# Seven quarter products in place of eight for the down products of three MLPs

## The chip, the core and the metric

The kernel runs on one NeuronCore of a Trainium2 chip as a single program. The metric is the device time of one execution in microseconds, from runs of the same program. Five engines work side by side, each through its own list of instructions in order: TensorE (PE, matmuls, with its weight loads shown apart as PEld), VectorE (DVE), ScalarE (ACT), GpSimd (POOL) and SyncE (SP, which here only issues DMAs).

## The reference

The reference is a small stack of transformer blocks on 512 tokens of width 1024, all in float32: a gated linear recurrence, a differential attention, a state-space mixer beside a windowed attention, and a cross attention. Three of the blocks end in an MLP, and only these matter here:

```python
def squared_relu_mlp(h, w_up, w_down):
    u = jax.nn.relu(h @ w_up)
    return (u * u) @ w_down
```

`w_up` is 1024 x 4096 and `w_down` 4096 x 1024. The first two MLPs are followed by an RMS norm with a gain and added to the residual; the third is added to the residual directly, and a last norm follows.

## The kernel before

Every large matrix product is made from float32 operands that are split in two rounded parts, high and low (type fp32r). `mm3` (line 398) multiplies a pair by a pair with three matmuls: high by high, high by low, low by high. For a split, ACT rounds the source to the high part and DVE subtracts it from the source to get the low part: `Weights._split` (lines 119 and 121) for weights, `split` (lines 407 and 408) for activations.

Weights pass through the class `Weights` (line 64). `specs` lists every unit of weights in the order of use; a unit is cut in parts of 128 x 1024 elements (512 KB). SP loads a part into one of three raw buffers, and the split writes one of six `hl` buffers. When the program asks for unit i (`get`, line 148), `ahead` splits parts until six of them from the start of unit i on are under way, and loads three parts further. An up unit and each half of a quarter product below is two parts.

`mlp` (line 586) treats the 4096 features in four blocks of 1024. In a block, four up units give 8 tiles of 128 features by 512 tokens: 24 matmuls of 128x128 against 128x512 each, into a PSUM buffer of the pool `ps_m` (three banks). `up_evac` takes the relu on ACT into `rl`, the square on DVE into `sq`, and splits it into the stationary operands `uk(0)` to `uk(7)`, which lie in `UAh`, `UAl`, `UBh` and `UBl`. Then the block's down product follows. For the first three blocks it is `tok2` (line 539), once for each half of the 1024 output columns: for each of four token tiles, 8 k steps of `mm3` into one PSUM buffer, and `add_to` (line 563) adds the result to `acc` or, in the third MLP, to `h` (in the first block of the first two MLPs ACT copies it):

```python
for u in range(2):
    cs = slice(u * 512, (u + 1) * 512)
    tok2(WT.get(f"{pre}dn{q}{u}"), uk, lambda t, ps: add_to(dst[:, t, cs], ps, post and q == 0))
```

The fourth block does the first half of its features in the same way and ends with `last_rows` (line 549), token tile by token tile, so that the norm that follows (`after`) can begin. `load_gp` (line 569) loads the gain row of that norm into the buffer `GP`, issued by ACT ahead of the MLP.

The order of instructions on each engine isn't the order of the program text. The framework plays the program against its own model of time when it builds it and lists for each engine, at each moment, the earliest instruction of the text that is ready in that model. On the chip each list then runs strictly in order, with semaphore waits.

Of the kernel before, what the change touches and what calls it, by code (L numbers as in the profile page):

```python
# [66 lines left out]
class Weights:  # L67


    def __init__(s, nc, raw_p, spl_p, specs, live, raws):  # L70
        s.nc, s.raw_p, s.spl_p, s.specs, s.live, s.raws = nc, raw_p, spl_p, specs, live, raws
        s.half = [(i, j) for i, sp in enumerate(specs) for j in range(s._parts(sp))]
        s.first = []
        n = 0
        for sp in specs:
            s.first.append(n)
            n += s._parts(sp)
        s.first.append(n)
        s.raw, s.hl = {}, {}
        s.n_dma = s.n_spl = s.n_get = 0  # L80
# [6 lines left out]
    @staticmethod  # L87
    def _rows(sp):
        return min(sp[1], 1024 // sum(c[3] for c in sp[2]))

    def _dma(s, q):
        i, j = s.half[q]
        name, nk, cols = s.specs[i][:3]
        w = sum(c[3] for c in cols)
# [11 lines left out]
        s.raw[q] = v  # L106

    def _split(s, q):
# [3 lines left out]
        w = sum(c[3] for c in cols)  # L112
        r = s.raw.pop(q)
# [25 lines left out]
    def load(s, n):  # L139
        for i in range(n):  # L140
            s._dma(s.n_dma)
            s.n_dma += 1
# [55 lines left out]
def body(ctx, tc, I, out, dbg=None, stop=None):  # L198
# [39 lines left out]

    def mlp_specs(pre, up, down):
# [158 lines left out]
    def mm3(ps, a, b, first, last):  # L398
        nc.tensor.matmul(ps, a[0], b[0], start=first, stop=False)  # L399
        nc.tensor.matmul(ps, a[0], b[1], start=False, stop=False)  # L400
        nc.tensor.matmul(ps, a[1], b[0], start=False, stop=last)  # L401
# [27 lines left out]
    def ev_y():  # L429
        return st["ev"].tile([P, D], F32, tag="y", name="y")  # L430
# [155 lines left out]
    def mlp(pre, post, after):  # L586
        wk = st["wk"]
        wk.phase()
        dst = acc if post else h

        def up_evac(u):
            def f(n, ps):
# [3 lines left out]
                sq = wk.get("sq", 512, 3)  # L596
# [3 lines left out]

        for q in range(4):
            us = 0
            if q == 0:
                i0 = WT.n_get
                ws = [WT.get(f"{pre}up00"), WT.get(f"{pre}up01", hold=i0)]
                feat_first(ws, xk, [up_evac(0), up_evac(1)])
                us = 2
            for u in range(us, 4):
                feat(WT.get(f"{pre}up{q}{u}"), xk, up_evac(u))
# [267 lines left out]
    load_gp(I["mlp_norm_post"][0])  # L877
# [10 lines left out]
    mlp("m0", True, after1)  # L888
# [149 lines left out]
    load_gp(I["mlp_norm_post"][1])  # L1038
# [13 lines left out]
    mlp("m1", True, after3)  # L1052
# [471 lines left out]
    load_gp(I["norm_final_2"])  # L1524
# [17 lines left out]
    mlp("m2", False, after6)  # L1542
# [30 lines left out]
```

## Time and profile before

| | us |
|---|---|
| median of three runs | 2620.57 (2620.28 to 2620.72) |
| the profiled execution | 2621.18 |
| its span, first to last instruction | 2619.3 |

| engine | busy us | share of the span | instructions |
|---|---|---|---|
| PE | 2552.2 | 97% | 13064 |
| PEld | 2130.0 | 81% | 13064 |
| DVE | 1481.6 | 57% | 2841 |
| ACT | 1142.4 | 44% | 2136 |
| POOL | 184.9 | 7% | 199 |

Busy time counts the time in which an engine has at least one instruction under way. Matmuls overlap each other, so the sum of their durations is larger than PE's busy time, and what a matmul costs is read from the distance of starts. Waits are listed with the instruction that ended them. 249.79 MB were moved by DMA.

### The profile page before, as it was taken

How to read it: one execution, taken by the hardware profiler on the slowest of the kernel's cores; microseconds unless marked ns; L12 is line 12 of the kernel's file. 1: busy time of each engine (PE TensorE's matmuls, PEld its weight loads, DVE VectorE, ACT ScalarE, POOL GpSimd, SP SyncE). 2: the span in 40 equal slices, each digit the busy share in tenths (PEclk: the TensorE clock that was granted, in tenths of full speed). 3: DMA queues.
4: the chain of work that ended last, by engine and by line, in shares of the span. 5: the costliest groups of instructions: out<-in, count | busy, mean ns of one | idle time of the engine just before them, and what ended most of it. 6: DMA issues, size and time to landing. Idle time of an engine off the chain costs nothing. (4 is left out here: it accounts for less than half of the span.)

```text
span 2619.3 us, 33641 instructions
## 1 busy us (share of the span) xinstructions
PE 2552.2 (97%) x13064; PEld 2130.0 (81%) x13064; DVE 1481.6 (57%) x2841; ACT 1142.4 (44%) x2136; POOL 184.9 (7%) x199
## 2 busy tenths in 40 slices
PE   8999999999999989999999999998999999999998
PEld 7888788888888768888887778787887788888887
DVE  5566653344666654333477788887555466534434
ACT  6333343233466553322356654563555336423322
POOL 1100210000201030000031100010000000100000
PEclk9999999999999999999999999998999999999999
DMA  5522233223222122332333433352221233222221
GB/s 179 154 65 65 81 105 96 88 96 99 88 89 89 65 89 88 105 95 82 105 117 112 110 105 109 104 145 79 72 73 32 89 97 121 81 97 97 97 97 57
DMA packets 187310, 249.79 MB, mean 95 GB/s; under 512 B 9936, under 2 KB 126912, under 8 KB 187152
## 3 DMA queue, kind: packets, MB, share of 16 engines
q1 hardware_dynamic: 175664, 207.97, 25.2%
q0 software_dynamic: 10192, 34.96, 5.0%
q10 hardware_dynamic: 1296, 4.72, 0.5%
q8 instruction: 103, 1.69, 0.3%
q14 instruction: 55, 0.45, 0.1%
HBM read 243.25 MB, written 9.61 MB: 97 GB/s over the span
## 5 line engine op out<-in xcount | busy, mean ns | idle before, releaser
L400 PE MATMUL psm<-XTl,hl 128*128 128x512 f32 (+1 forms) x1400 | 537.6, 384 | 7.8 <-DVE XTl L408 7.8
L399 PE MATMUL psm<-XTh,hl 128*128 128x512 f32 (+1 forms) x1400 | 534.8, 383 | 5.9 <-ACT XTh L407 5.1
L401 PE MATMUL psm<-XTh,hl 128*128 128x512 f32 (+1 forms) x1400 | 534.5, 382 | 0.0
L119 ACT ACTIVATE hl<-raw 128x1024 fp32r<-128x1024 f32 x321 | 338.4, 1056 | 425.5 <-PE psm L401 361.3
L121 DVE TENSOR_TENSOR hl<-raw,hl 128x1024 fp32r<-128x1024 f32 x305 | 374.9, 1231 | 247.9 <-ACT hl L119 244.8
L400 PEld LDWEIGHTS psm<-XTl,hl 128*128 128x128 f32 x1400 | 266.9, 191 | 57.1 <-DVE XTl L408 8.6
L399 PEld LDWEIGHTS psm<-XTh,hl 128*128 128x128 f32 x1400 | 266.0, 190 | 55.4 <-ACT XTh L407 6.1
L401 PEld LDWEIGHTS psm<-XTh,hl 128*128 128x128 f32 x1400 | 266.6, 190 | 48.8 <-issue 0.2
L399 PE MATMUL psm<-hl,UAh 128*128 128x512 f32 x640 | 255.9, 400 | 5.0 <-DVE WS L1130 1.8
L400 PE MATMUL psm<-hl,UAh 128*128 128x512 f32 x640 | 251.0, 392 | 0.0
L401 PE MATMUL psm<-hl,UAl 128*128 128x512 f32 x640 | 251.0, 395 | 0.0
L399 PE MATMUL psm<-hl,XTh 128*128 128x512 f32 (+1 forms) x640 | 231.2, 362 | 4.1 <-ACT XTh L407 3.2
L400 PE MATMUL psm<-hl,XTh 128*128 128x512 f32 (+1 forms) x640 | 229.8, 359 | 0.0
L401 PE MATMUL psm<-hl,XTl 128*128 128x512 f32 (+1 forms) x640 | 229.2, 358 | 0.0
L399 PE MATMUL psm<-hl,UBh 128*128 128x512 f32 (+1 forms) x512 | 202.2, 395 | 1.2 <-ACT UBh L410 0.8
L400 PE MATMUL psm<-hl,UBh 128*128 128x512 f32 (+1 forms) x512 | 200.6, 392 | 0.0
L401 PE MATMUL psm<-hl,UBl 128*128 128x512 f32 (+1 forms) x512 | 198.4, 390 | 0.0
L597 DVE TENSOR_TENSOR WK<-WK,psm 128x512 f32<-128x512 f32 x90 | 61.8, 687 | 171.4 <-ACT WK L595 171.4
L595 ACT ACTIVATE WK<-psm 128x512 f32<-128x512 f32 x90 | 53.9, 599 | 226.7 <-PE psm L401 226.7
L567 DVE TENSOR_TENSOR ACC<-psm,ACC 128x512 f32<-128x512 f32 x112 | 75.9, 686 | 134.9 <-PE psm L401 134.5
L399 PEld LDWEIGHTS psm<-hl,UAh 128*128 128x128 f32 x640 | 121.1, 189 | 33.7 <-DVE ACC L567 3.0
L401 PEld LDWEIGHTS psm<-hl,UAl 128*128 128x128 f32 x640 | 120.5, 188 | 27.0 <-issue 0.7
(415 smaller groups left out, 4016.0 us busy)
## 6 DMA issues: line engine op xcount, KB each, us to landing
raw<-in_mlp_w_up_dram SPq DMA_DIRECT2D x64, 512.0 KB, 3.9
raw<-in_mlp_w_down_dram SPq DMA_DIRECT2D x64, 512.0 KB, 3.3
raw<-in_w_in_dram SPq DMA_DIRECT2D x60, 512.0 KB, 3.7
WS<-aD POOLq DMA_DIRECT2D x32, 512.0 KB, 6.1
raw<-in_w_up_dram SPq DMA_DIRECT2D x32, 512.0 KB, 3.7
raw<-in_w_down_dram SPq DMA_DIRECT2D x32, 512.0 KB, 3.6
raw<-in_w_in_dram SPq DMA_DIRECT2D x33, 256.0 KB, 3.2
raw<-in_a_w_in_dram SPq DMA_DIRECT2D x16, 512.0 KB, 5.6
```

The source lines that it names most:

```text
L119: s.nc.scalar.activation(out=h, in_=r, func=AF.Copy)
L121: eng.tensor_tensor(out=l, in0=r, in1=h.bitcast(F32), op=ALU.subtract)
L399: nc.tensor.matmul(ps, a[0], b[0], start=first, stop=False)
L400: nc.tensor.matmul(ps, a[0], b[1], start=False, stop=False)
L401: nc.tensor.matmul(ps, a[1], b[0], start=False, stop=last)
L567: nc.vector.tensor_tensor(out=dst, in0=ps, in1=dst, op=ALU.add)
L595: nc.scalar.activation(out=rl, in_=ps, func=AF.Relu)
L597: nc.vector.tensor_tensor(out=sq, in0=rl, in1=ps, op=ALU.mult)
```

## The change

For the first three blocks of each MLP, the down product C = A B (A: 512 tokens x 1024 features, B: 1024 features x 1024 columns) is cut in quarters A11 to A22 and B11 to B22, and the four quarters of C come from seven products of quarters:

- P1 = A11 B11; P2 = A12 B21
- P5 = (A22 - A21)(B11 + B12); P6 = (A21 - A22 - A11)(B11 + B12 + B22)
- P7 = (A11 - A21)(B12 + B22); P3 = (A22 - A21 + A11 - A12) B22
- P4 = A22 (B11 + B12 + B22 + B21)
- C11 = P1 + P2; C22 = -P5 - (P1 + P6 + P7); C12 = -(P1 + P6) - (P5 + P3); C21 = P1 + P6 + P7 + P4

They run in the order 1, 5, 6, 2, 7, 3, 4. A product is 2 token tiles of 128 by 512 columns over 4 k steps. Products 1, 6, 7 and 4 add on in the same two PSUM banks ("a", from the pool `ps_s`), 5 and 3 in two others ("b"), and 2 has two of `ps_m` ("c"); after each product its banks are read and added to or subtracted from a quarter of `dst`.

The squares stay unsplit in `U` (4096 words of the work buffer `WK`). `left(p)` forms the left operand of product p in place in `U` on DVE where it is a sum (products 5, 6, 7 and 3) and splits it into one of `UAh`, `UAl`, `UBh`, `UBl` in turn, two parts of 1024 in each. The first is made ahead of the third up unit, three more at the start of the down product, and the others after the products 1, 5 and 6.

For the weights, each product is a unit of two parts (j = 0, 1). Products 1, 5, 2, 7 and 4 load a part into a raw buffer as before. `_hold` loads B11 into `T` (a buffer of the pool `ev` for each j) for product 5 and B22 into `B22` or `GP` for product 6, issued by SP up to five parts ahead of the raw loads. `_combine` adds the raw part to `T` (products 5 and 4), B22 to `T` (product 6) or B22 to the raw part (product 7), on DVE, before the split. As `GP` is in use, `load_gp` moves to the end of the third block.

```diff
@@ class Weights
+    def _hold(s, q):
+        u = s._sums(q)
+        if u is None:
+            return
+        (ap, k0), p = u
+        j = s.half[q][1]
+        need = {5: ((0, 0, 0),), 6: ((2, 1, 1),)}.get(p, ())
+        for (r, kh, ch) in need:
+            t = s.place(r, j)
+            r0 = (k0 + 4 * kh + 2 * j) * P
+            s.nc.sync.dma_start(
+                out=t.rearrange("p (k n) -> p k n", k=2),
+                in_=ap[r0:r0 + 2 * P, ch * 512:(ch + 1) * 512].rearrange("(k p) n -> p k n", p=P))
+            s.held[r, j] = t
+    def _combine(s, q):
+        (_, p), j = s._sums(q), s.half[q][1]
+        add = lambda a, b: s.nc.vector.tensor_tensor(out=a, in0=a, in1=b, op=ALU.add)
+        T = s.held.get((0, j))
+        if p == 6:
+            add(T, s.held[2, j])
+            return T
+        if p == 3:
+            return s.held[2, j]
+        r = s.raw.pop(q)
+        if p in (5, 4):
+            add(T, r)
+            return T
+        if p == 7:
+            add(r, s.held[2, j])
+        return r
...
     def load(s, n):
         for i in range(n):
+            while s.n_held < min(s.n_dma + 5, s.first[-1]):
+                s._hold(s.n_held)
+                s.n_held += 1
             s._dma(s.n_dma)
...
+    SEVEN = ((1, (0, 0)), (5, (0, 1)), (6, None), (2, (1, 0)), (7, (0, 1)), (3, None), (4, (1, 0)))
...
             if q < 3:
-                wide(f"{pre}dn{q}", down, q * 8, 8)
+                seven(f"{pre}dn{q}", down, q * 8)
...
-    def mlp(pre, post, after):
+    def held(r, j):
+        if r == 0:
+            return ev_y()
+        return st["GP"] if j else st["B22"]
+    def mlp(pre, post, after, gp):
...
+        U = wk.get("U", 4096).rearrange("p (k n) -> p k n", k=8)
+        st["B22"] = wk.get("B22", 1024) if post else ACC[:, 0:1024]
...
+        def up_keep(u):
+            def f(n, ps):
+                rl = wk.get("rl", 512, 3)
+                nc.scalar.activation(out=rl, in_=ps, func=AF.Relu)
+                nc.vector.tensor_tensor(out=U[:, u * 2 + n], in0=rl, in1=ps, op=ALU.mult)
+            return f
...
+        def left(p):
+            a11, a12, a21, a22 = (quarter(*i) for i in ((0, 0), (0, 1), (1, 0), (1, 1)))
+            stt = lambda o, x, y: nc.vector.scalar_tensor_tensor(out=o, in0=x, scalar=-1.0, in1=y, op0=ALU.mult, op1=ALU.subtract)
+            if p == 5:
+                nc.vector.tensor_tensor(out=a21, in0=a22, in1=a21, op=ALU.subtract)
+            elif p == 6:
+                stt(a11, a21, a11)
+            elif p == 7:
+                stt(a21, a11, a22)
+            elif p == 3:
+                stt(a12, a11, a12)
...
+            split((h_, l_), {1: a11, 5: a21, 6: a11, 2: a12, 7: a21, 3: a12, 4: a22}[p])
+            return h_, l_
+        def down7(q):
+            order = [p for p, _ in SEVEN]
+            lefts = [left(p) for p in order[1:4]]
+            lefts.insert(0, st.pop("left1"))
+            banks = {}
+            plan = {1: ("a", ((0, 0, 1),)), 5: ("b", ((1, 1, -1),)), 6: ("a", ((0, 1, -1),)), 2: ("c", ((0, 0, 1),)),
+                    7: ("a", ((1, 1, -1),)), 3: ("b", ((0, 1, -1),)), 4: ("a", ((1, 0, 1),))}
+            written = set() if post and q == 0 else {(i, j) for i in range(2) for j in range(2)}
+            for n, p in enumerate(order):
+                w = WT.get(f"{pre}dn{q}s{p}")
+                lh, ll = lefts[n]
+                b, outs = plan[p]
+                new = b not in banks
+                if new:
+                    banks[b] = [PM() if b == "c" else PS() for i in range(2)]
+                for i in range(2):
+                    ps = banks[b][i]
+                    tk = slice(i * P, (i + 1) * P)
+                    for k in range(4):
+                        mm3(ps, (lh[:, k, tk], ll[:, k, tk]), w[k], new and k == 0, k == 3, True)
+                    for (r, c, sg) in outs:
+                        d = dst[:, 2 * r + i, 512 * c:512 * c + 512]
+                        if (r, c) not in written:
+                            nc.scalar.activation(out=d, in_=ps, func=AF.Copy, scale=float(sg))
+                        else:
+                            nc.vector.tensor_tensor(out=d, in0=d, in1=ps, op=ALU.add if sg > 0 else ALU.subtract)
+                written |= {o[:2] for o in outs}
+                if n + 4 < 7:
+                    lefts.append(left(order[n + 4]))
...
             if q < 3:
-                for u in range(2):
-                    cs = slice(u * 512, (u + 1) * 512)
-                    tok2(WT.get(f"{pre}dn{q}{u}"), uk, lambda t, ps: add_to(dst[:, t, cs], ps, post and q == 0))
+                down7(q)
+                if q == 2:
+                    load_gp(gp)
```

The fourth block, the up products, the norms and all other stages stay as they are.

## Rows read from the trace of the kernel before

**Rows 1.** The page's first part: busy us (share of the span) x instructions, by engine.
```profile
PE 2552.2 (97%) x13064; PEld 2130.0 (81%) x13064; DVE 1481.6 (57%) x2841; ACT 1142.4 (44%) x2136; POOL 184.9 (7%) x199
```
**Rows 2.** The page's chain that ended last: shares by engine, then by line.
```profile
PE 30%; DVE 0%; ACT 0%; issue 0%; ACTq 0%
PE psm L399 8%; PE psm L400 8%; PE psm L401 8%; PE pss L1374 2%; PE pss L1370 1%; PE pss L1349 1%; PE pss L492 0%; PE pss L1491 0%; PE pss L401 0%; PE pss L400 0%; PE pss L399 0%; PE pss L1485 0%; PE pss L1423 0%; DVE h L567 0%; DVE XTl L408 0%
```
**Rows 3.** Stretches: us; busy (count) of PE, PEld, DVE, ACT, POOL; clock; DMA share; GB/s.
```profile
431.00:474.60 43.60, 43.60 (x194) 36.05 (x193) 20.11 (x23) 17.03 (x23) 0.00 (x0) 1.00 0.36 119
474.60:518.90 44.30, 44.30 (x193) 36.06 (x192) 14.89 (x17) 9.50 (x10) 0.00 (x0) 1.00 0.25 73
```
**Rows 4.** Timeline of ACT: start, duration, instruction, count, idle time before and releaser.
```profile
386.69 0.60 ACT L595 ACTIVATE WK<-psm 128x512 f32<-128x512 f32 x1 [1.72 <-PE psm L401]
...
404.63 1.06 ACT L119 ACTIVATE hl<-raw 128x1024 fp32r<-128x1024 f32 x1 [0.79 <-PE psm L401]
...
408.80 0.60 ACT L565 ACTIVATE ACC<-psm 128x512 f32<-128x512 f32 x1 [0.29 <-PE psm L401]
...
431.01 0.60 ACT L565 ACTIVATE ACC<-psm 128x512 f32<-128x512 f32 x1 [0.34 <-PE psm L401]
...
474.62 0.60 ACT L595 ACTIVATE WK<-psm 128x512 f32<-128x512 f32 x1 [1.72 <-PE psm L401]
```
**Rows 5.** Groups by line and form: count, busy us, mean ns, idle before, releasers.
```profile
L121 DVE TENSOR_TENSOR hl<-raw,hl 128x1024 fp32r<-128x1024 f32 x304 | 372.7, 1227 | 247.9 <-ACT hl L119 244.8
L119 ACT ACTIVATE hl<-raw 128x1024 fp32r<-128x1024 f32 x320 | 337.8, 1057 | 425.5 <-PE psm L401 361.3 <-DMA raw<-in_mlp_w_up_dram 24.8 <-DMA raw<-in_w_up_dram 13.3
L597 DVE TENSOR_TENSOR WK<-WK,psm 128x512 f32<-128x512 f32 x90 | 61.8, 687 | 171.4 <-ACT WK L595 171.4
L407 ACT ACTIVATE UBh<-WK 128x512 fp32r<-128x512 f32 x48 | 30.1, 627 | 18.1 <-DVE WK L597 18.1
L579 DVE SCALAR_TENSOR_TENSOR h<-WK,rr,h 128x1024 f32<-128x1024 f32 x3 | 3.8, 1279 | 0.2
```
**Rows 6.** Timeline of DVE, up and down stretches of the first MLP.
```profile
358.73 1.23 DVE L121 TENSOR_TENSOR hl<-raw,hl 128x1024 fp32r<-128x1024 f32 x1 [1.21 <-ACT hl L119]
359.87 0.69 DVE L408 TENSOR_TENSOR UAl<-WK,UAh 128x512 fp32r<-128x512 f32 x1
360.48 0.68 DVE L597 TENSOR_TENSOR WK<-WK,psm 128x512 f32<-128x512 f32 x1
...
493.65 2.60 DVE L121 TENSOR_TENSOR hl<-raw,hl 128x1024 fp32r<-128x1024 f32 x2 [1.79 <-ACT hl L119]
...
497.61 0.68 DVE L567 TENSOR_TENSOR ACC<-psm,ACC 128x512 f32<-128x512 f32 x1
```
**Rows 7.** Busy time by stretch: the kernel's start, and a wait before the first MLP.
```profile
0.00:65.00 65.00, 55.91 (x340) 50.60 (x341) 36.50 (x85) 42.22 (x91) 11.88 (x28) 1.00 0.58 180
340.00:350.00 10.00, 10.00 (x74) 10.00 (x74) 7.35 (x15) 4.15 (x10) 0.00 (x0) 0.84 0.30 108
```
**Rows 8.** DMA issue: count, KB each, median us from issue to landing.
```profile
raw<-in_mlp_w_up_dram SPq DMA_DIRECT2D x64, 512.0 KB, 3.9
```
**Rows 9.** Who waited for whom: us in total, times, longest.
```profile
SPq L101 <- DVE hl L121: 1603.3, 266, 62.5
...
DVE hl L121 <- ACT hl L119: 244.8, 186, 15.6
```
**Rows 10.** Timeline of PE after a wait, shortly before the first MLP.
```profile
337.45 0.58 PE L400 MATMUL psm<-XTl,hl 128*128 128x256 f32 x1 [3.20 <-DVE XTl L408]
337.83 0.41 PE L401 MATMUL psm<-XTh,hl 128*128 128x256 f32 x1
338.04 0.41 PE L399 MATMUL psm<-XTh,hl 128*128 128x256 f32 x1
...
343.35 0.28 PE L401 MATMUL psm<-XTh,hl 128*128 128x256 f32 x1
343.47 0.28 PE L399 MATMUL psm<-XTh,hl 128*128 128x256 f32 x1
```

More of the change, by code (lines that the diff above doesn't have):

```diff
@@ L79, in __init__ @@
         s.raw, s.hl = {}, {}
-        s.n_dma = s.n_spl = s.n_get = 0
+        s.n_dma = s.n_spl = s.n_get = s.n_held = 0
+        s.held = {}
     @staticmethod
@@ L88, in _rows, with _sums @@
     def _rows(sp):
-        return min(sp[1], 1024 // sum(c[3] for c in sp[2]))
+        return min(sp[1], 1024 // sum(c[3] for c in sp[2])) if sp[2] else 2
+    def _sums(s, q):
+        sp = s.specs[s.half[q][0]]
+        return sp[4] if len(sp) > 4 else None
+    def _hold(s, q):
[28 more added lines that the diff above has]
+        return r
     def _dma(s, q):
@@ L93, in _dma @@
         name, nk, cols = s.specs[i][:3]
+        if not cols:
+            return
         w = sum(c[3] for c in cols)
@@ L105, in _dma @@
             o += n
-        s.raw[q] = v
+        s.raw[q] = raw if s._sums(q) else v
     def _split(s, q):
@@ L111, in _split @@
         gain = s.specs[i][3] if len(s.specs[i]) > 3 else None
-        w = sum(c[3] for c in cols)
-        r = s.raw.pop(q)
+        if s._sums(q):
+            r = s._combine(q).rearrange("p (k n) -> p k n", k=2)
+            w = 512
+        else:
+            w = sum(c[3] for c in cols)
+            r = s.raw.pop(q)
         kp = s._rows(s.specs[i])
@@ L237, in lastk, with seven @@
             specs.append((f"{name}{u}", 2, [(ap, k0 + u // 2 * 2, 512 * (u % 2), 512)]))
+    SEVEN = ((1, (0, 0)), (5, (0, 1)), (6, None), (2, (1, 0)), (7, (0, 1)), (3, None), (4, (1, 0)))
+    def seven(name, ap, k0):
+        for p, b in SEVEN:
+            cols = [] if b is None else [(ap, k0 + 4 * b[0], 512 * b[1], 512)]
+            specs.append((f"{name}s{p}", 4, cols, None, ((ap, k0), p)))
     def mlp_specs(pre, up, down):
@@ L396, in xk, with mm3 @@
         return XTh[:, k], XTl[:, k]
[L398 to L401, printed above, removed]
+    def mm3(ps, a, b, first, last, partial=False):
+        nc.tensor.matmul(ps, a[0], b[0], start=first, stop=False, skip_group_check=partial)
+        nc.tensor.matmul(ps, a[0], b[1], start=False, stop=False, skip_group_check=partial)
+        nc.tensor.matmul(ps, a[1], b[0], start=False, stop=last, skip_group_check=partial)
     def split(dst, src, scale=None):
@@ L589, in mlp @@
         dst = acc if post else h
+        WT.place = held
+        U = wk.get("U", 4096).rearrange("p (k n) -> p k n", k=8)
+        st["B22"] = wk.get("B22", 1024) if post else ACC[:, 0:1024]
         def up_evac(u):
@@ L601, in mlp @@
         for q in range(4):
             us = 0
+            keep = up_keep if q < 3 else up_evac
             if q == 0:
@@ L605, in mlp @@
                 ws = [WT.get(f"{pre}up00"), WT.get(f"{pre}up01", hold=i0)]
[L606 removed]
+                feat_first(ws, xk, [keep(0), keep(1)])
                 us = 2
             for u in range(us, 4):
[L609 removed]
+                if u == 2 and q < 3:
+                    st["left1"] = left(1)
+                feat(WT.get(f"{pre}up{q}{u}"), xk, keep(u))
             if q < 3:
[L611 to L613 removed]
+                down7(q)
+                if q == 2:
+                    load_gp(gp)
             else:
@@ L887, in body @@
     norm_places(0, 3)
-    mlp("m0", True, after1)
+    mlp("m0", True, after1, I["mlp_norm_post"][0])
     if stop == "mlp0":
```

15 lines of the change are left out of this document (9 added, 6 removed).

## The prediction
> **What bounds the kernel now.** The first thing to read is the table of busy time: PE is busy 97% of the span, DVE 57%, ACT 44% [rows 1]. The chain that ended last is, by engine, PE and next to nothing else, with the three matmul lines of `mm3` in front [rows 2]. Shares over the whole span are not enough for a change that touches one kind of stage, so the next view is that stage: the table by stretches over the MLP of layer 0 [rows 3]. In the down stretch (474.60 to 518.90) PE is busy 44.30 of 44.30 us and in the up stretch ahead of it 43.60 of 43.60, both at clock 1.00, while DVE is busy 14.89 us in the down stretch and 20.11 in the up stretch. So nothing but the number of matmuls sets the end there, and the vector engine has more than half of each stretch free.
>
> The cadence comes from the timeline of ACT. The last up result of a block leaves PSUM at 386.69 and the last down result at 431.01 [rows 4]: 44.32 us for the 192 matmuls between, 0.2308 us each. The four results from 408.80 to 431.01 give 22.21/96 = 0.2314. The up stretch, with as many matmuls, gives 43.60/192 = 0.2271. A matmul's own duration is longer than its turn (0.41 against 0.21 us in the first of [rows 10]), because matmuls overlap; it is not used.
>
> **Removed.** A block's down product is 2 column halves x 4 token tiles x 8 k x 3 = 192 matmuls. After the change it is 7 products x 2 token tiles x 4 k x 3 = 168, of the same shape (128x128 against 128x512). That is 24 fewer in each of 3 x 3 = 9 blocks: 24 x 0.2308 = 5.54 us a block, 49.9 us in all (49.1 by 0.2271, 50.0 by 0.2314). Nothing stood beside PE that could take this time over unless one of the added steps does, so these decide.
>
> **Added on DVE and ACT.** Rows of the kinds of instruction are [rows 5]: 1.227 us for 128x1024 from SBUF to SBUF, 0.687 for a 128x512 read of PSUM, 1.279 for a scalar_tensor_tensor of 1024, and 1.057 (ACT) for a 1024 conversion. The adds of raw weights have no row; the subtraction L121 has the same shape and reads two F32 operands in SBUF, so I take its 1.227; the bounds are 0.69, were an add of 1024 as quick as a 512 read, and the 1.279 of L579, which would move the 8 adds by 4 us a block or by half a microsecond. Per block, before: 16 weight subtractions, 8 squares, 8 subtractions of U, 8 results = 16 x 1.227 + 24 x 0.687 = 36.1 us; the two stretches show 20.11 + 14.89 = 35.0. After: 22 weight subtractions (8 up, 14 down), 8 adds of weights, 7 subtractions and 4 sums of the left operands, 8 squares, 14 results = 37 x 1.227 + 4 x 1.279 + 22 x 0.687 = 65.6 us, in a block that lasts 43.6 + 38.8 = 82.4 us. Over the block DVE rises from 40% to 80%: it fits. ACT gains 6 + 7 conversions of 1024 and loses 8 of 512: 13 x 1.057 - 8 x 0.627 = +8.7 us on 26.5 (17.03 + 9.50): it fits as well.
>
> The narrow place is the down stretch. Only the left operand of the first product is formed early; six left operands, the weights from the third product on, those of the next two up units and all results are asked for inside it: 14 weight subtractions, 6 weight adds, 6 subtractions and 4 sums on the left, 14 results = 26 x 1.227 + 4 x 1.279 + 14 x 0.687 = 46.6 us. Back to back an instruction costs less than its duration: 1.23 us ones start 1.14 apart and 0.69 ones 0.60 apart [rows 6]. With 0.085 off each of 44 that is 42.9 us, more than PE's 168 x 0.2308 = 38.8. Two things bring it under. The adds need no split buffer, only their loads, so the two of the third product and one of the fifth can be made in the up stretch, where DVE idles more than half the time (3 x 1.14 = 3.4 us); and the second up unit's weights and the last four results aren't needed before the next up stretch (2 x 1.14 + 4 x 0.60 = 4.7 us). That leaves 34.8 us in 38.8. This counts on an order in which later work is not stuck behind a wait. The timelines show that order: at 493.65 DVE subtracts weights of a unit two ahead, before the result that stands first in the program and comes at 497.61 [rows 6], and ACT converts at 404.63 before the result of 408.80 [rows 4]. If that cover were gone, DVE sets the stretch: 42.9 us.
>
> **Deadlines.** The first product is ready early. The second needs the last up result: relu 0.60 [rows 4] and square 0.69, so 1.3 us after the last matmul, then its sum 1.23, conversion 1.06, subtraction 1.23: 4.8 us, due after one product, 24 x 0.2308 = 5.54. The third is due at 11.1 and its sum follows at once. So it is met with 0.7 us to spare in the narrowest place.
>
> **Banks.** Four of the seven products add on in the same two PSUM banks, after DVE (or ACT) has read them. Between two of these always stands one other product, so a read has 5.54 us to happen in, and takes 0.69: the sum counts nothing. Were all three reads a block in the way of PE, it would be 3 x 0.69 x 9 = 19 us, 2593, which lies between the forecast and the first rival and is counted there. The Trainium skill ("Perfetto Trace Analysis", section "Matmuls") speaks against the scheme: independent groups should rotate through PSUM banks, so that evacuation overlaps the next group. By it the 19 us would be due; no row of before has one accumulation that comes back to a bank after a read, so neither is shown.
>
> **Loads.** A block loads 22 pieces of 512 KB, not 16: 11.5 MB in 82.4 us, 140 GB/s, where the stretches show 73 to 119 [rows 3]. The first 65 us of the kernel moved 180 GB/s with the DMA engines 0.58 busy [rows 7], and a piece lands 3.9 us after issue [rows 8]. The six more stand in SP's queue, where raw loads wait for a free buffer anyway (1603 us in 266 waits [rows 9]); the loads of held blocks wait for readers that end over an up unit earlier. Cost nothing; with that cover gone, one load of 3.9 us a block, 35 us. The gain row's load moves behind the third block, still an up and a down stretch ahead of its reader: nothing, and the wait for GP's last reader has only ACT's queue behind it. The up stretch gets lighter (8 ACT and 8 DVE instructions fewer): no gain, PE has no wait there.
>
> **The sum.** For stalls I take 0.4 us a block, nearer to nothing (the deadlines are met) than to the 4.1 of a DVE-bound stretch (42.9 - 38.8): 3.6 us. The profiled execution took 2621.2 us (span 2619.3): 2621.2 - 49.9 + 3.6 = 2574.9. The median of the three runs is 0.6 lower, so I predict 2574. A difference under 0.2%, 5 us, can't be told from none.
>
> **The rivals.**
> *DVE becomes the bound of the down stretch.* Nothing can be done ahead or put off, and it lasts 42.9 us: 44.3 - 42.9 = 1.4 a block, 13 us in all, 2608. For it: 42.9 against 38.8. Against it: the rows of reordering. Anything between the two cases counts here too.
>
> *The clock falls.* At 337.45 PE had waited 3.20 us for DVE; from 337.83 on matmuls of 256 columns start 0.21 apart, and only from 343.35 on 0.12 apart [rows 10]: 5.52 us hold 26 turns, which would have taken 3.1; the granted clock of 340 to 350 is 0.84, a mix of 1.2 and 2.4 GHz [rows 7]. One such wait a block costs 3.2 + 2.4 = 5.6 us, 50 in nine blocks: 2621, no change. This needs a wait of that length, and the worst I find is that of a stretch bound by DVE, 4.1 us, if it came in one piece. The Trainium skill ("TensorE: Matmul & The Clock Gate", section "A second HAM failure mode: psum-queue depth-cycling") has a kernel whose short idles between groups of banks made the clock oscillate; the wait at 337 bears it out for long waits, and for short ones no row shown here does.
>
> *Slower: DVE waits inside its own chains.* Each sum is added on DVE, converted on ACT and subtracted on DVE. If the order written for DVE puts nothing between, it stands still for 1.06 us in each of the 10 sums of a down stretch (6 of weights, 4 left): 42.9 + 10.6 = 53.5, 9.2 more than 44.3, +83 us: 2703. It turns slower than before from 1.4 us of such waiting a stretch. For it: DVE waits for ACT's conversions 244.8 us in 186 waits already [rows 9]. Against it: that is time when it had nothing else to do.
>
> **Chances.** Forecast 0.68 (its own range 2569 to 2585: the saving with no stall and 2 us off for what I can't see, up to 1.6 us a block). DVE-bound 0.20, clock 0.05, slower chains 0.07. Range 2568 to 2610: the first two cases. Faster 0.88, same 0.05, slower 0.07.
>
> **What would show it.** Right: down stretches of 38.8 to 39.5 us with PE busy throughout, clock 1.00, DVE busy over 85% in them; up stretches still 43.6. DVE as bound: PE waits at the third or fifth product, released by a weight subtraction or a left sum. Clock: under 1.00 in down stretches. Chains: idle time of DVE before the subtractions, released by ACT, inside the down stretches. Wrong altogether: a down stretch over 44.3 us, or waits of PE for loads.

## The result, and the profile after

| | median us | runs | profiled execution |
|---|---|---|---|
| before | 2620.64 | 4 (2620.28 to 2621.27) | 2621.18 |
| changed | 2582.36 | 4 (2581.61 to 2584.00) | 2581.83 |

The ratio is 0.9855, with an interval of 0.9837 to 0.9872: 38.3 us less, where 46.6 were forecast. All of it comes from the nine down stretches. I measure one from the last up result on ACT to the second up result of the next block, less the 10.88 us that the 48 matmuls in between take at 0.2267 us. Before, that gives 44.35 us, against 44.32 to the last down result by [rows 4], and 399.2 in all nine. After, two of them last 39.3 and 39.4 us (the first block of the first two MLPs, where ACT makes 8 of the results and DVE has 8 instructions less), the other seven 40.2 to 40.3: 360.35 in all, 38.9 less.

This measure counts on PE doing the next block's up matmuls tile by tile. In the long blocks of e4, e7 and e9 below it doesn't quite: 218 matmuls start before that second up result, against 215 in the changed kernel, and the stretch reads some 0.5 us too long. So a second sum stands beside it, of nine whole blocks: from the last up result of a block to the last of the next, which takes in a down product and the next block's up product, whatever their order. By the timelines of ACT, first after the change and then in e9, from the second block of the first MLP to the third:

```profile
469.19 0.60 ACT L671 ACTIVATE WK<-psm 128x512 f32<-128x512 f32 x1 [1.73 <-PE psm L459]
...
553.03 0.60 ACT L671 ACTIVATE WK<-psm 128x512 f32<-128x512 f32 x1 [1.73 <-PE psm L459]
```

```profile
468.63 0.60 ACT L672 ACTIVATE WK<-psm 128x512 f32<-128x512 f32 x1 [1.61 <-PE psm L459]
...
550.76 0.60 ACT L672 ACTIVATE WK<-psm 128x512 f32<-128x512 f32 x1 [1.62 <-PE psm L459]
```

That is 83.84 us after the change and 82.13 in e9; before, from the first block to the second, it was 87.93 ([rows 4], 386.69 to 474.62). The nine together fall from 791.4 to 752.6 us, 38.8 less.

The first part of the page and the chain that ended last, of the changed kernel, beside [rows 1, 2]:

```profile
PE 2504.9 (97%) x12848; PEld 2088.2 (81%) x12848; DVE 1714.5 (66%) x3048; ACT 1220.2 (47%) x2181; POOL 183.5 (7%) x199
...
PE 28%; DVE 2%; ACT 0%; issue 0%; ACTq 0%
```

PE has 216 matmuls less, the 9 x 24 of the forecast, and is still the chain. But DVE, which had 0% of it, now has 2%: work that PE waits for. The stretches show where, in the same MLP as [rows 3], with the same columns:

```profile
425.60:469.20 43.60, 43.60 (x194) 36.06 (x193) 22.75 (x22) 14.22 (x19) 0.00 (x0) 1.00 0.35 109
469.20:509.40 40.20, 39.19 (x169) 31.37 (x168) 37.56 (x39) 20.43 (x20) 0.00 (x0) 1.00 0.52 169
```

The up stretch is the same 43.60 us. In the down stretch PE is busy 39.19 of 40.20 us, at clock 1.00, and DVE 37.56, 93%. The missing 1.0 us of PE lies in two waits, which the timeline of PE in that stretch shows (idle time before an instruction and its releaser in brackets):

```profile
474.52 0.39 PE L457 MATMUL pss<-hl,UAh 128*128 128x512 f32 x1
...
475.21 0.40 PE L458 MATMUL pss<-hl,UAh 128*128 128x512 f32 x1
475.44 0.63 PE L457 MATMUL psm<-hl,UBh 128*128 128x512 f32 x2
476.92 0.50 PE L457 MATMUL pss<-hl,UAl 128*128 128x512 f32 x1 [0.84 <-ACT UAl L465]
477.25 0.40 PE L458 MATMUL pss<-hl,UAl 128*128 128x512 f32 x1
477.49 0.40 PE L459 MATMUL pss<-hl,UAh 128*128 128x512 f32 x1
...
492.98 0.50 PE L458 MATMUL pss<-hl,UAh 128*128 128x512 f32 x1 [0.17 <-DVE hl L167]
```

In this block the left operand of product 5 lies in `UAh`, of 6 in `UAl`, of 2 in `UBh`. After product 1 PE can do four matmuls of product 5 (L457 and L458 need only the high part) and two of product 2. Then its list goes on with product 6, whose high part (the releaser named) ends at 476.87, and with L459 of product 5, whose low part ends at 476.91 (both below): it stands until 476.92. It loses about 1.0 us of matmul turns here, and 0.1 more since the next start comes 0.33 and not 0.23 us later. The second wait, 0.2 to 0.36 us and 0.1, is for the low part of product 3's weights. The first wait is in all nine blocks (0.6 us in the two short ones), the second in seven.

### The profile page after: what moved, and what is told of

It is laid out like the page before. It is cut to its first block, busy times and chain, and to the rows that moved or that the text cites. A ratio compares the mean times of both kernels' runs of the same rounds, so it can differ in the third digit from the quotient of the medians.

```text
span 2580.1 us, 33650 instructions
## 1 busy us (share of the span) xinstructions
PE 2504.9 (97%) x12848; PEld 2088.2 (81%) x12848; DVE 1714.5 (66%) x3048; ACT 1220.2 (47%) x2181; POOL 183.5 (7%) x199
## 5 line engine op out<-in xcount | busy, mean ns | idle before, releaser
L458 PE MATMUL psm<-XTl,hl 128*128 128x512 f32 (+1 forms) x1400 | 537.3, 384 | 7.8 <-DVE XTl L466 7.8
L457 PE MATMUL psm<-XTh,hl 128*128 128x512 f32 (+1 forms) x1400 | 534.5, 382 | 5.9 <-ACT XTh L465 5.1
L459 PE MATMUL psm<-XTh,hl 128*128 128x512 f32 (+1 forms) x1400 | 533.3, 382 | 0.0
L165 ACT ACTIVATE hl<-raw 128x1024 fp32r<-128x1024 f32 x303 | 319.3, 1056 | 313.9 <-PE psm L459 132.6
L167 DVE TENSOR_TENSOR hl<-raw,hl 128x1024 fp32r<-128x1024 f32 x287 | 352.7, 1233 | 149.0 <-ACT hl L165 147.9
L458 PEld LDWEIGHTS psm<-XTl,hl 128*128 128x128 f32 x1400 | 266.3, 190 | 56.9 <-DVE XTl L466 8.6
L457 PEld LDWEIGHTS psm<-XTh,hl 128*128 128x128 f32 x1400 | 265.9, 190 | 55.7 <-ACT XTh L465 6.1
L459 PEld LDWEIGHTS psm<-XTh,hl 128*128 128x128 f32 x1400 | 266.3, 190 | 48.5
L457 PE MATMUL psm<-hl,XTh 128*128 128x512 f32 (+1 forms) x640 | 231.1, 362 | 4.4 <-ACT XTh L465 3.3
L458 PE MATMUL psm<-hl,XTh 128*128 128x512 f32 (+1 forms) x640 | 229.9, 359 | 0.1
L459 PE MATMUL psm<-hl,XTl 128*128 128x512 f32 (+1 forms) x640 | 229.1, 358 | 0.0
L457 PE MATMUL psm<-hl,UAh 128*128 128x512 f32 x368 | 148.6, 405 | 4.9 <-DVE ACC L625 1.5
L458 PE MATMUL psm<-hl,UAh 128*128 128x512 f32 x368 | 144.9, 395 | 0.0
L459 PE MATMUL psm<-hl,UAl 128*128 128x512 f32 x368 | 143.7, 396 | 0.0
L457 PEld LDWEIGHTS psm<-hl,XTh 128*128 128x128 f32 x640 | 122.3, 191 | 21.8 <-ACT XTh L465 3.7
L458 PEld LDWEIGHTS psm<-hl,XTh 128*128 128x128 f32 x640 | 122.2, 191 | 16.6 <-issue 0.5
L459 PEld LDWEIGHTS psm<-hl,XTl 128*128 128x128 f32 x640 | 122.3, 191 | 15.9 <-issue 0.5
L671 ACT ACTIVATE WK<-psm 128x512 f32<-128x512 f32 x66 | 39.5, 598 | 160.8 <-PE psm L459 160.8
L457 PE MATMUL psm<-hl,UBh 128*128 128x512 f32 (+1 forms) x240 | 93.5, 391 | 1.1 <-ACT UBh L468 0.8
L459 PE MATMUL psm<-hl,UBl 128*128 128x512 f32 (+1 forms) x248 | 94.3, 388 | 0.0
L1257 DVE SCALAR_TENSOR_TENSOR WS<-psm,CW,WS 128x511 f32<-128x511 f32 (+1 forms) x120 | 87.5, 740 | 8.7 <-ACT WS L1253 8.4
L458 PE MATMUL psm<-hl,UBh 128*128 128x512 f32 (+1 forms) x240 | 92.2, 386 | 0.0
```

The source lines that it names most:

```text
L165: s.nc.scalar.activation(out=h, in_=r, func=AF.Copy)
L167: eng.tensor_tensor(out=l, in0=r, in1=h.bitcast(F32), op=ALU.subtract)
L457: nc.tensor.matmul(ps, a[0], b[0], start=first, stop=False, skip_group_check=partial)
L458: nc.tensor.matmul(ps, a[0], b[1], start=False, stop=False, skip_group_check=partial)
L459: nc.tensor.matmul(ps, a[1], b[0], start=False, stop=last, skip_group_check=partial)
L671: nc.scalar.activation(out=rl, in_=ps, func=AF.Relu)
```

## The experiments

Two readings of the waits were set against each other. A: what counts is the place, that is, the DVE instructions that stand in the list ahead of the one that PE needs. B: what counts is the amount of DVE work in the down stretch, whatever its order. For runs that move adds to GpSimd there is a third, C: POOL's adds slow DVE down. The two sums are over the nine down stretches and the nine whole blocks, measured as above; the difference is to the kernel before, run on the same chip beside it.

| run | us | to before | nine stretches | nine whole blocks | waits of PE in a stretch |
|---|---|---|---|---|---|
| before | 2620.64 | | 399.2 | 791.4 | none |
| changed | 2582.36 | -38.3 | 360.4 | 752.6 | 1.0 and 0.3 |
| e1_k7 | 2574.50 | -47.2 | 350.3 | 742.6 | none |
| e2_no_left_sums | 2567.58 | -54.1 | 346.9 | 739.1 | none |
| e3_no_weight_adds | 2582.01 | -39.7 | 357.1 | 749.0 | 1.0 |
| e4_order | 2577.17 | -44.6 | 357.0 | 745.7 | 0.8, at another place |
| e5_pool_adds | 2616.42 | -2.9 | 390.7 | 782.6 | 1.0 and 2.25 to 2.95 |
| e6_order_pool | 2605.32 | -14.0 | 385.0 | 776.9 | up to 2.4 |
| e7_order_early7 | 2571.66 | -47.7 | 350.5 | 739.6 | none |
| e8_order_pool4 | 2585.41 | -34.0 | 363.4 | 755.2 | 1.3 and 0.5 |
| e9_best | 2569.86 | -51.9 | 351.0 | 739.5 | none |
| e10_two_more_down | 2593.18 | -28.6 | 374.3 | 766.5 | 1.8 to 2.4 |
| e11_two_more_up | 2581.58 | -40.2 | 360.3 | 752.6 | 1.0 and 0.3 |

Runs e2, e3, e5, e6, e10 and e11 are single executions; those of e4, which was run four times, lie up to 4.3 us apart. Outside the nine blocks the traces span 1824.9 to 1832.0 us from run to run, so the sums are the better measure of these edits.

**e1: the matmuls alone.** The kernel before with 7 of 8 k steps in the same down products, so 168 matmuls a block and nothing added.

```diff
-                    tok2(WT.get(f"{pre}dn{q}{u}"), uk, lambda t, ps: add_to(dst[:, t, cs], ps, post and q == 0))
+                    tok2(WT.get(f"{pre}dn{q}{u}"), uk, lambda t, ps: add_to(dst[:, t, cs], ps, post and q == 0), n_k=7)
```

> The kernel before, with the last of the eight k steps left out of the down products of the first three blocks of each MLP: the same 216 matmuls fewer as in the change, and nothing added (the output then lacks an eighth of these products). It measures the saving by itself. Theory A (the saving is 216 x 0.231 = 49.9 us, and the change gave 11 us of it back in two waits of PE a block, one of about 1.0 us for a late left operand 6.7 us into the down stretch and one of 0.33 us for a late weight part at 23.5 us): 2620.6 - 49.9 = 2570.7 us. Rival B (a removed matmul is worth less than its turn, since the stretch is held by something else too): above 2576 us, with waits of PE that the kernel before doesn't have.

Ratio 0.9821 (0.9804 to 0.9837). The stretch that answers to the second of [rows 3]:

```profile
474.60:513.50 38.90, 38.90 (x170) 31.62 (x169) 14.58 (x16) 8.49 (x8) 0.00 (x0) 1.00 0.32 101
```

All nine last 38.93 us, PE busy throughout. So in this form 24 matmuls are worth 44.35 - 38.93 = 5.42 us a block, 48.8 in all, and against it the changed kernel gives back 360.35 - 350.34 = 10.0 us in its stretches. Against e2 and e9, which run the 168 matmuls in the changed kernel's own seven products and without a wait of PE, it gives back more in whole blocks: 752.59 - 739.10 = 13.5 us and 752.59 - 739.55 = 13.0 us. That is the quantity to explain. Why e1 takes 0.3 to 0.4 us a block longer than these two with the same number of matmuls was not looked into.

**e2: no left sums.** The four sums of `left` are left out; the operands are split as they are.

```diff
-            if p == 5:
+            if p < 0:
...
-            elif p == 6:
+            elif p == -6:
...
-            elif p == 7:
+            elif p == -7:
...
-            elif p == 3:
+            elif p == -3:
```

> The changed kernel without the four sums of the left operands (products 5, 6, 7 and 3 take the quarter as it is; the products are then other ones): 4 x 1.14 = 4.6 us of DVE a block less, and 1.2 us out of the chain from the last up result to the second and third product. Theory A (the chain is late): the first wait of a block falls from 1.0 us to under 0.3, 9 x 0.8 to 1.0 us, so 2573 to 2575 us. Theory B (DVE has too little time in the whole down stretch, whatever the chain): both waits go, 2571 to 2573 us. The two differ in the second wait (0.33 us at 23.5 us of the stretch): A keeps it, B loses it.

Both waits go, with 4 x 1.2 us taken out of the DVE line. The second is named for a weight, so the narrow A of this expectation, the left operand's own chain, is out. The wider A above is not: all four sums stand in DVE's list ahead of that weight part, which DVE makes at 491.71 in the changed kernel. So e2 doesn't part A from B.

**e3: no weight adds.** `_combine` adds nothing.

```diff
-        add = lambda a, b: s.nc.vector.tensor_tensor(out=a, in0=a, in1=b, op=ALU.add)
+        add = lambda a, b: None
```

> The changed kernel without the eight adds of weights a block (products 5, 6, 7 and 4 take the loaded part as it is; all loads stay): 8 x 1.14 = 9.1 us of DVE a block less, twice as much as the left sums, but none of it in the chain from the last up result to the second product. Theory A: the first wait of a block stays at 0.8 us or more, the second goes; 2578 to 2580 us. Theory B: both waits go, 2571 to 2573 us.

The first wait stays as it was and the second goes; the timeline of PE in the block shown above:

```profile
479.01 0.50 PE L457 MATMUL pss<-hl,UAl 128*128 128x512 f32 x1 [0.78 <-ACT UAl L465]
```

Eight adds a block less, more DVE time than the four sums of e2, and the first wait does not move: they do not stand ahead of it. For this wait that is A, and against B. The whole time isn't shorter in this single run although the nine blocks are 3.6 us shorter: the first MLP starts 2.3 us later. Why, I did not follow up.

**e4: another order.** Products 1, 2, 5, 6, 3, 7, 4, so that a product without a sum stands second.

```diff
-    SEVEN = ((1, (0, 0)), (5, (0, 1)), (6, None), (2, (1, 0)), (7, (0, 1)), (3, None), (4, (1, 0)))
+    SEVEN = ((1, (0, 0)), (2, (1, 0)), (5, (0, 1)), (6, None), (3, None), (7, (0, 1)), (4, (1, 0)))
```

> The changed kernel with the products in the order 1, 2, 5, 6, 3, 7, 4 in place of 1, 5, 6, 2, 7, 3, 4: the second product then needs a left operand that is a quarter as it is, without a sum, and the first sum is due one product (5.5 us) later; 7 and 4 then follow each other in the same banks. DVE, ACT, loads and matmuls are the same in number. Theory A: the first wait of a block goes (1.0 us and the slower restart, 1.25 us in all), the second stays or moves: 2571 to 2576 us. Theory B: the missing time shows up later in the stretch, 2580 to 2584 us. If the banks decide (product 4 has to wait for the results of 7), a new wait of 0.7 us or more stands before the last product.

Ratio 0.9834 (0.9819 to 0.9848). The first wait is gone, the two short blocks are free of waits (38.5 and 38.7 us), and in the seven others a new one of 0.7 to 0.9 us stands in product 7, the sixth in PE's list, and not before the last product, as the expectations of e6 to e8 have it. In this block the left operand of 7 lies in `UAh` and that of 4 in `UAl`. PE's timeline at that wait and at the start of product 4, and the last of the gapless line of DVE ahead of the wait:

```profile
495.84 0.50 PE L459 MATMUL pss<-hl,UAh 128*128 128x512 f32 x1 [0.51 <-DVE UAh L466]
...
507.32 0.39 PE L457 MATMUL pss<-hl,UAl 128*128 128x512 f32 x1
```

```profile
494.57 1.22 DVE L466 TENSOR_TENSOR UAh<-WK,UAh 128x1024 fp32r<-128x1024 f32 x1
495.71 0.68 DVE L722 TENSOR_TENSOR ACC<-ACC,pss 128x512 f32<-128x512 f32 x1
```

The instruction that PE waits for ends at 495.79 and was itself late for no wait: DVE starts one instruction after another from 468.81 on, 1.5 us into the stretch. So order moves the wait (A), and it comes back further down because the line is full (B): an operand is late by the DVE work ahead of it since the start of the stretch. A full line alone doesn't make a wait, as e9 shows below. The banks, the third possibility of the expectation, don't decide here: product 4, which adds on in the banks of 7, starts without a wait, with matmuls of the next up product ahead of it, and e7 and e9 have no wait with the same order of products. Over whole blocks the new order takes back 6.9 of the 13.0 us.

**e5, e6, e8: adds on GpSimd.** The remedy by B would be to take work off DVE. e5 moves all weight adds to GpSimd, e6 does so with the order of e4, e8 only those of product 4 with that order.

```diff
-        add = lambda a, b: s.nc.vector.tensor_tensor(out=a, in0=a, in1=b, op=ALU.add)
+        add = lambda a, b: s.nc.gpsimd.tensor_tensor(out=a, in0=a, in1=b, op=ALU.add)
```

```diff
-        add = lambda a, b: s.nc.vector.tensor_tensor(out=a, in0=a, in1=b, op=ALU.add)
+        add = lambda a, b: (s.nc.gpsimd if p == 4 else s.nc.vector).tensor_tensor(out=a, in0=a, in1=b, op=ALU.add)
```

> The changed kernel with the eight adds of weights a block on POOL instead of DVE. POOL's 128x1024 subtraction L121 took 2.64 us in the kernel before, so 21 us of POOL in a block of 83, and 9.1 us of DVE less. Theory A (two places a block, each held by what DVE has in front of it): as without the adds, the first wait stays at about 1.0 us and the second goes, nine down stretches of 357 us in all, about 2579 us. Rival C (POOL and DVE get in each other's way: before the first MLP a DVE subtraction of 1024 took 2.34 us beside a POOL instruction, against 1.23 alone): each of the 8 POOL adds stretches what DVE does beside it, up to 8 x 1.1 = 9 us a block, and the waits get longer: 2590 us or more, with DVE instructions of over 2 us in the down stretches.

> The order 1, 2, 5, 6, 3, 7, 4 and the adds on POOL together. With the order alone one wait of 0.7 to 0.9 us was left, before the last product, where DVE's line, without a gap from the start of the stretch, is late by that much. Theory A: 6 adds less in the stretch (6.8 us) are more than enough, no wait is left, down stretches of 38.5 us, 2565 to 2568 us. Rival C (POOL and DVE in each other's way): 2580 us or more.

> The order 1, 2, 5, 6, 3, 7, 4 with only the two adds of product 4 on POOL (the last ones in the stretch, with the most time): 2.3 us of DVE less in the stretch. Theory A: no wait before the last product, 2566 to 2570 us. Rival C: DVE instructions beside the two POOL adds take up to 1.1 us longer, the gain is lost: 2574 to 2580 us.

All three are slower than with the adds on DVE (e8: ratio 0.9868, 0.9851 to 0.9884, against 0.9834 of e4 with the same order): C. The timelines of POOL and of DVE in e5 show how:

```profile
483.78 4.04 POOL L116 TENSOR_TENSOR raw<-raw,GP 128x1024 f32<-128x1024 f32 x1 [15.67 <-DMA raw<-in_mlp_w_down_dram]
487.77 3.39 POOL L116 TENSOR_TENSOR y<-y,raw 128x1024 f32<-128x1024 f32 x1
```

```profile
486.07 2.83 DVE L167 TENSOR_TENSOR hl<-raw,hl 128x1024 fp32r<-128x1024 f32 x1
488.82 0.68 DVE L722 TENSOR_TENSOR ACC<-ACC,pss 128x512 f32<-128x512 f32 x1
489.42 2.83 DVE L466 TENSOR_TENSOR UAh<-WK,UAh 128x1024 fp32r<-128x1024 f32 x1
```

POOL's adds end at 487.82 and 491.16; the two DVE subtractions that started while they ran end at 488.90 and 492.25, 1.08 and 1.09 us later, so they did their work only after POOL had ended. They read two operands in SBUF. The result of 488.82, which reads one from PSUM, took its usual 0.68 us under a running POOL add. An add that costs 1.14 us in the DVE line costs it 2.83 - 1.22 = 1.6 us when it runs on POOL. The Trainium skill ("SBUF — State Buffer", section "SBUF: two separate sides") says that GpSimd and a DVE instruction with two SBUF inputs share a pair of ports as an exclusive lock: the one that starts first holds it for its whole instruction, and the other is blocked. These rows agree with it.

In e8 each of the 18 adds on POOL holds up one DVE instruction, which then takes 2.83 to 3.29 us, and one of these is what PE waits for. In the first MLP's second block it is the low part of product 6's left operand:

```profile
484.88 3.03 DVE L466 TENSOR_TENSOR UBh<-WK,UBh 128x1024 fp32r<-128x1024 f32 x1
```

```profile
487.96 0.50 PE L459 MATMUL pss<-hl,UBh 128*128 128x512 f32 x1 [0.98 <-DVE UBh L466]
```

Not all of e5's loss is this. Its nine blocks are 30.0 us longer than the changed kernel's: 2.3 to 2.5 us in each of four, and 3.9 to 4.15 in the five in which the granted clock fell after the wait. In e6, PE's second wait in the seven long blocks, 1.98 to 2.15 us, is named for a result. It stands before product 3, which adds on in the banks of product 5. In the same block:

```profile
495.75 0.47 PE L457 MATMUL pss<-hl,UBl 128*128 128x512 f32 x1 [1.98 <-DVE ACC L722]
```

**e7: one sum earlier.** The order of e4, and the sum of product 7, A11 - A21, made in the up stretch in a buffer `S7` of its own (both quarters are complete there), where DVE idles half of the time.

```diff
+        S7 = (wk.get("S7", 1024) if post else ACC[:, 1024:2048]).rearrange("p (k n) -> p k n", k=4)
...
-            elif p == 7:
-                stt(a21, a11, a22)
...
-            split((h_, l_), {1: a11, 5: a21, 6: a11, 2: a12, 7: a21, 3: a12, 4: a22}[p])
+            split((h_, l_), {1: a11, 5: a21, 6: a11, 2: a12, 7: S7, 3: a12, 4: a22}[p])
...
                     st["left1"] = left(1)
+                    nc.vector.tensor_tensor(out=S7, in0=quarter(0, 0), in1=quarter(1, 0), op=ALU.subtract)
```

> The order 1, 2, 5, 6, 3, 7, 4, and the sum of the left operand of product 7, A11 - A21, formed directly from the first two up units, in the up stretch, into a buffer of its own, in place of a sum in the down stretch. The same number of instructions; one DVE instruction of 1.14 us moves out of the down stretch. Theory A: the wait of 0.7 to 0.9 us before the last product goes, or falls under 0.2; down stretches of 38.5 to 38.9 us, 2565 to 2570 us. Theory D (the wait there is not DVE's line but the weight add in front of the last left operand, which waits for its load): the wait stays, 2575 to 2578 us.

Ratio 0.9815 (0.98 to 0.9829). The new wait of e4 is gone as well, so theory D is out; stretches of 38.5 to 39.1 us. The nine whole blocks take 739.6 us, against 739.1 in e2, which makes no sums: the loss is taken back. In this run `S7` lies over a gain row of a later norm, which then computes something else; e9 mends that.

**e9: the same with room for the buffer.** The relu is written into `U` and squared in place there, so that `rl` is not needed.

```diff
-                rl = wk.get("rl", 512, 3)
+                rl = U[:, i]
...
-                rl = wk.get("rl", 512, 3)
+                rl = U[:, u * 2 + n]
```

> The order 1, 2, 5, 6, 3, 7, 4 and the early sum A11 - A21 as in the run before, which had put its extra buffer so that a gain row of a later norm was overwritten; now the relu is written into U and squared in place, so that the buffer rl goes and there is room. Same instructions on all engines. Theory A: down stretches of 38.5 to 39.1 us without a wait of PE, 2568 to 2573 us, 9 to 14 us under the changed kernel. Theory E (the square in place makes the conversion of the next up result wait, or up stretches get longer): up stretches over 43.6 us, 2574 us or more.

The same two stretches as above, of e9:

```profile
425.08:468.63 43.55, 43.55 (x193) 36.00 (x192) 22.90 (x23) 15.46 (x19) 0.00 (x0) 1.00 0.39 129
468.63:507.73 39.10, 39.10 (x172) 31.97 (x171) 36.71 (x39) 20.02 (x20) 0.00 (x0) 1.00 0.44 145
```

The up stretch is not longer, so theory E is out. In the down stretch PE is busy 39.10 of 39.10 us, beside a DVE that is busy 36.71, 94% of it. Ratio to before 0.9798 (0.9785 to 0.9812), which lies clear of the changed kernel's 0.9855 (0.9837 to 0.9872): this version beats both. Of the 13.6 us between the two, 13.0 lie in the nine whole blocks; the stretches show 9.3 of them, since they read too long for this order.

**e10, e11: the suspected cause doubled.** The changed kernel with two more adds of 128x512 on DVE, once at the start of each down product, once in the up stretch behind `left(1)` (there on `U[:, 2]` and `U[:, 3]`).

```diff
+            for _ in range(2):
+                nc.vector.tensor_tensor(out=wk.get("X", 512), in0=U[:, 6], in1=U[:, 7], op=ALU.add)
```

> The changed kernel with two more DVE instructions of 128x512 (an add of two tiles of U into a place that nobody reads) at the start of each down product, first in the program's order there: 2 x 0.60 = 1.2 us of DVE more a block, on nothing that PE needs. Theory A (PE's first wait is as long as what stands in DVE's line ahead of the second and third left operand): the first wait grows from 1.0 to about 2.2 us, +11 us, 2592 us. Theory F (the wait belongs to the chain of the operand itself, and DVE has room around it): no change, 2582 us.

> The same two DVE instructions, but in the middle of each block's up stretch, where DVE is idle for over a third of the time. By every theory that puts the loss into the down stretch: no change, 2582 us, first wait 1.0 us. If DVE is full over the whole block: +5 us or more.

In the up stretch they cost nothing: sum 360.3, waits unchanged. At the start of the down stretch the first wait grows from 1.0 us to between 2.2 and 2.36 (1.75 in the two short blocks), by the 2 x 0.6 us that two such instructions take in the line. What DVE does ahead of the late operand comes out at this wait one for one. The whole run is 10.8 us above the changed kernel, but that this is 9 x 1.2, as expected, is chance: the nine blocks are 13.9 us longer. In three of the seven long ones they grow by only 0.7 to 0.9 us, since the second wait goes, and the two short ones by 1.0 to 1.1; in the other four the clock fell too, and they grow by 2.2 to 2.5. Timeline of PE and two stretches (us; busy (count) of PE, PEld, DVE, ACT, POOL; clock; DMA share; GB/s):

```profile
476.97 0.80 PE L457 MATMUL pss<-hl,UAl 128*128 128x512 f32 x1 [2.04 <-ACT UAl L465]
477.57 0.63 PE L458 MATMUL pss<-hl,UAl 128*128 128x512 f32 x1
477.99 0.63 PE L459 MATMUL pss<-hl,UAh 128*128 128x512 f32 x1
...
563.04 0.50 PE L457 MATMUL pss<-hl,UAh 128*128 128x512 f32 x1 [2.07 <-ACT UAh L465]
563.38 0.40 PE L458 MATMUL pss<-hl,UAh 128*128 128x512 f32 x1
```

```profile
477.60:480.60 3.00, 3.00 (x9) 2.39 (x8) 3.00 (x3) 0.00 (x0) 0.00 (x0) 0.55 0.24 68
563.40:566.40 3.00, 3.00 (x14) 2.42 (x13) 3.00 (x4) 0.00 (x0) 0.00 (x0) 1.00 0.11 29
```

After the first wait the granted clock is 0.55 for 3 us (mostly the lower level, 1.2 GHz), with starts 0.43 us apart; after one as long in the next block it is 1.00 and they start 0.23 apart.

## Why the prediction was right, and which term was off

**Removed: right within 4%.** 49.9 us were forecast. e1 measured 48.8, where a turn takes 0.2317 us in the stretch of 168 and 0.2310 in that of 192. In the changed kernel's own products, without a wait, the nine blocks of e9 are 791.40 - 739.55 = 51.9 us shorter than before, 5.76 a block against the forecast 5.54.

**Prices of the added instructions: right.** The adds that had no row took 1.220 us (1.227 taken from L121), the scalar_tensor_tensor 1.217 (1.279 taken), a result 0.679 (0.687). These groups by line, of the changed kernel from 340 to 640 us, answer to [rows 5]:

```profile
L722 DVE TENSOR_TENSOR ACC<-ACC,pss 128x512 f32<-128x512 f32 x28 | 18.6, 679 | 3.5 <-PE pss L459 3.5
...
L116 DVE TENSOR_TENSOR y<-y,raw 128x1024 f32<-128x1024 f32 x12 | 14.6, 1220 | 7.5 <-DMA raw<-in_mlp_w_down_dram 7.4
...
L681 DVE SCALAR_TENSOR_TENSOR WK<-WK 128x1024 f32<-128x1024 f32 x9 | 11.0, 1217 | 0.0
```

**DVE in the down stretch: fits, but with less room than the sum gave.** I had it at 34.8 us in 38.8, and it is busy 37.56 in 40.20, in a line without a gap from 0.6 us after the start of a stretch to about 37 us. One weight subtraction and two results that I had put off to the up stretch are done inside it, and the last square, which that sum did not have. It is under the time of PE, as e9 shows with 36.71 in 39.10 and no wait, so the first rival, DVE as the bound at 2608, did not come; what I called "anything between the two cases" did, at the near end. By my own signs the forecast case itself did not come: it asked for stretches of 38.8 to 39.5 us with PE busy throughout, and seven of nine last 40.2 to 40.3 with two waits.

**Deadlines: the step that failed.** The stalls were put at 0.4 us a block, 3.6 in all. Against e9, with the same added work and no wait, they came to 13.0: 1.5 to 1.7 in each of seven blocks, 0.7 to 0.8 in the other two (10.0 against e1). The saving was 2 us larger than forecast and the stalls 9.4 larger, so part of the miss was offset; the result lies in the forecast's own range because that left up to 1.6 us a block for what it couldn't see. The prediction said that the second product's left operand is ready 4.8 us after the last up matmul, due at 5.54, "with 0.7 us to spare in the narrowest place". It was ready 7.7 us after. The timeline of DVE from the last up result (469.19) on, beside [rows 6]:

```profile
469.82 0.69 DVE L672 TENSOR_TENSOR WK<-WK,psm 128x512 f32<-128x512 f32 x1 [1.10 <-ACT WK L671]
470.55 1.22 DVE L683 TENSOR_TENSOR WK<-WK 128x1024 f32<-128x1024 f32 x1
471.69 1.22 DVE L167 TENSOR_TENSOR hl<-y,hl 128x1024 fp32r<-128x1024 f32 x1
472.82 1.22 DVE L466 TENSOR_TENSOR UBh<-WK,UBh 128x1024 fp32r<-128x1024 f32 x1
473.96 0.68 DVE L722 TENSOR_TENSOR ACC<-ACC,pss 128x512 f32<-128x512 f32 x1
474.56 1.22 DVE L681 SCALAR_TENSOR_TENSOR WK<-WK 128x1024 f32<-128x1024 f32 x1
475.69 1.22 DVE L466 TENSOR_TENSOR UAh<-WK,UAh 128x1024 fp32r<-128x1024 f32 x1
```

and of ACT, beside [rows 4]:

```profile
469.19 0.60 ACT L671 ACTIVATE WK<-psm 128x512 f32<-128x512 f32 x1 [1.73 <-PE psm L459]
...
470.64 1.05 ACT L465 ACTIVATE UBh<-WK 128x1024 fp32r<-128x1024 f32 x1
471.80 1.06 ACT L465 ACTIVATE UAh<-WK 128x1024 fp32r<-128x1024 f32 x1
...
475.81 1.06 ACT L465 ACTIVATE UAl<-WK 128x1024 fp32r<-128x1024 f32 x1
```

The square (L672) and the sum (L683) start when the prediction has them, and the conversion to `UAh` starts as soon as the sum ends and is done at 472.86, on time: that of product 2 (`UBh`), which stands ahead of it on ACT, ends at 471.69. Then the low part of `UAh`, for which the 4.8 us allowed one subtraction, starts at 475.69 and not at 472.86: DVE first has the low part of product 2, a result and the sum of product 6 to do, in an order fixed in advance. So each link was priced right and the chain was wrong as a sum: each was counted as if it had its engine to itself, in a stretch where the same prediction had DVE busy for nine tenths. e4 (product 2 put second) and e10 (two instructions more ahead of it) show that this place is what costs. The prediction also worked out one deadline only, that of the second product; the second wait, and the one of e4, fall at later operands of the same full line (e2, e4, e7).

**Banks: right for the changed kernel.** Nothing was counted for products that return to a bank after a read, against the Trainium skill ("Perfetto Trace Analysis", section "Matmuls"), by which 19 us might be due. PE's waits in the MLPs of the changed kernel name splits of operands, never a result (L722): no such cost shows. It comes due where DVE is late: in e6, with POOL's adds in the way, seven waits of about 2 us are named for a result, although product 6 stands between the two that share the banks, 5 and 3. The 5.54 us that the prediction gave a read hold only while DVE's list reaches it in time.

**Loads and gain row: right.** The down stretch moves 169 GB/s where it moved 73, and no wait of PE in the MLPs has a DMA as its releaser.

**The clock: not here, but near.** It stays at 1.00 through the down stretches of the changed kernel, with waits of 1.0 us. With 1.2 us more (e10), and with 2.25 to 2.95 (e5), the case of the second rival begins, in some blocks.

**DVE waiting inside its own chains (the slower side): no.** The line has no gap while it matters; between a sum and its subtraction other work always stands. That is the same fact which broke the deadline: what keeps DVE busy in a chain's waiting time is what makes the chain longer.

## What to carry to other kernels

When a change fills a second engine to nine tenths of a stretch, check each deadline of the first engine against everything that stands in the second one's list ahead of it, and not against the chain alone; the average only says that it fits. Put first the pieces that need no preparation, and move a piece whose inputs are early out of the full stretch: one reordered tuple and one sum moved took the whole loss back (13.0 us in nine blocks). An engine that idles is no free helper if it blocks the one that it is to relieve: time one instruction beside the other engine first.

## What the runs showed of the hardware that I had not expected

- A fp32 add of 1024 on POOL blocks a DVE instruction with two SBUF operands until it ends, 1.22 us becoming 2.83, and leaves one that reads a PSUM operand at 0.68 (e5). In e5, e6 and e8 there are 115 DVE instructions of 1024 that outlast a POOL add, and all end 1.08 to 1.09 us after it, whenever they started; the 74 with a PSUM operand that started under one took 0.67 to 0.69.
- Waits of the same length can have a different price. In e10, 2.04 us was followed by 3 us at clock 0.55 and 2.07 us by full clock; over all, the lower clock followed in 4 of the 7 long blocks of e10, whose wait lost 2.2 to 2.4 us of turns, in 5 of 9 of e5 (2.25 to 2.95) and in 2 of the 7 long ones of e6 (2.15 to 2.45). In no block whose longest wait was 0.6 to 1.8 us did it. e5 in two neighbouring blocks, timeline of PE:

```profile
497.91 0.50 PE L458 MATMUL pss<-hl,UAh 128*128 128x512 f32 x1 [2.74 <-DVE hl L167]
498.25 0.39 PE L459 MATMUL pss<-hl,UAh 128*128 128x512 f32 x1
498.48 0.40 PE L457 MATMUL pss<-hl,UAh 128*128 128x512 f32 x1
...
584.13 0.50 PE L458 MATMUL pss<-hl,UBl 128*128 128x512 f32 x1 [2.75 <-DVE hl L167]
...
585.47 0.63 PE L457 MATMUL pss<-hl,UBl 128*128 128x512 f32 x1
585.90 0.63 PE L458 MATMUL pss<-hl,UBl 128*128 128x512 f32 x1
```

What decides between them was not tried.
